# Attention products with values: one matmul over all query tiles for a head's first two key tiles, with three raw weight buffers for four

## The chip, the cores and the metric

The kernel runs on one core of one Trainium2 chip. The metric is device time in microseconds (us) of that core. TensorE (PE, with its weight loads PEld), VectorE (DVE), ScalarE (ACT) and GpSimd (POOL) each take their instructions in a fixed order; SyncE (SP) issues most of the transfers.

## The reference, cut to what matters

Two residual layers over 512 tokens of width 1024, all in float32. The change lies in layer 0, whose mixer has two halves that read one normalised input: gated linear attention (GLA, 4 heads) and block-sparse softmax attention (MoBA, 8 heads of width 64).

```python
def mix_even(h, w_in, w_gate2, b_gate, gla_norm, q_norm, k_norm, w_o):
    proj = h @ w_in
    qa, ka, va, ra, glr, qb, kb, vb = _split(proj, EVEN_SPLITS)
    ...
    oa = rmsnorm(gla_chunked(...), gla_norm).reshape(B, S, GLA_V) * jax.nn.silu(ra)
    ob = moba_attention(rmsnorm(qb, q_norm), rmsnorm(kb, k_norm), vb)
    return jnp.concatenate([oa, ob], axis=-1) @ w_o
```

With 512 tokens and blocks of 256, a MoBA head is softmax over the causal keys of a 512 by 512 score matrix (with a penalty on one block), times the values.

## The kernel before, in words

Activations lie transposed: 128 channels on the partitions, 512 tokens along a row. To keep float32 accuracy every large product is made of three matmuls (`mm3`, L130 to L132), on a high and a low part of each operand. Weights arrive as blocks of 128 x 1024; each lands in a `raw` buffer, ACT casts it into `whi` (L114), and DVE takes the rest into `wlo` (L115).

A MoBA head h has, for its two query halves g = 0 and 1 (two query tiles of 128 each):
- S(h, g) (`s_step`): the scores, and the softmax on DVE, ACT and POOL, which leaves probabilities `p`.
- T(h, g, jj) (`t_step`): PE transposes of the blocks of `p` for the key tiles 2jj and 2jj+1 into the one PSUM bank `ptp`; ACT casts them to the high part of `th`, DVE subtracts for the low part (L711, L712).
- A(h, g, jj) (`a_step`): the products of values and `th` into the one bank `av` (L726). After the last one ACT copies half of `av` to `lo` (L732) and DVE adds into `of` (L733); every second head casts `of` into the operand A (L735, L736).

The three T and the three A of a head are (0,0), (1,0) and (1,1). Between these steps PE does "fills", pieces of six 512-wide matmuls of other projections (`fill`): in order qa, ka, va, the gate's halves ra0 and ra1, and the output projection wob. The class `Plan` decides the order when the program is built: each step has a cost, dependencies with assumed latencies (`LAT`) and PSUM banks; it takes the first step that is due by its own clock, and a fill where none is. PE's order on the chip is this order; it waits where a step comes too early.

When ra0 or ra1 is done, a chain makes its gate `sl` for two 512-wide halves, one after the other through one buffer `ra` (xin[:, 7]): DVE multiplies (L627), ACT does Exp, Ln, Exp (L628 to L630), POOL multiplies (L631); the second half's DVE step waits for the first half's POOL step.

After the MoBA heads comes the GLA stage, planned likewise, for n = 0 to 7: `att` (L799 to L801) makes scores in two `s` banks, which DVE copies under a mask into `atts` (L802); `kt` transposes keys, which ACT copies to `kst` (L810); `ds` (L819) needs `kst`; `o` needs the copied `atts`; ACT normalises its result `ob` (L840 to L850); `otp` (L860) transposes it, and DVE multiplies it by `sl` (L862). The buffers `atts` and `sts` are cleared on POOL (L783, L786), whose order puts these clears behind both multiplies of ra0's gate:

```python
pool.tensor_mul(s1, s1, ra)                 # L631, in ra_g(0), then ra_g(1)
a = gl.tile([P, 2, 2, P], F32, name=f"att{p}")
pool.memset(a, 0.0)                         # L783
```

Of the kernel before, what the change touches and what calls it, by code (L numbers as in the profile page):

```python
# [7 lines left out]
F32 = mybir.dt.float32  # L8
F32R = mybir.dt.float32r
U32 = mybir.dt.uint32  # L10
AF = mybir.ActivationFunctionType
ALU = mybir.AluOpType
AX = mybir.AxisListType

P = 128
S = 512
# [28 lines left out]
def kernel(  # L45
# [13 lines left out]
    act, dve, pool, pe = nc.scalar, nc.vector, nc.gpsimd, nc.tensor  # L59

    cp = ctx.enter_context(tc.tile_pool(name="cp", bufs=1))
    wp = ctx.enter_context(tc.tile_pool(name="wp", bufs=4))
# [21 lines left out]
    A = cp.tile([P, 32, S], F32R, name="A")  # L84
    ident = cn[:, C_ID : C_ID + P]
# [11 lines left out]
    def m_tile(name, tag="tp"):  # L97
        return ps.tile([P, S], F32, tag=tag, name=name, bufs=2 if tag == "s" else 1)
# [5 lines left out]
    def block_parts(n):  # L104
        i = wcount[0]
        wcount[0] += 1
        raw = wp.tile([P, 1024], F32, tag="raw", name=f"raw{i}", bufs=4)
        hi = wp.tile([P, 1024], F32R, tag="whi", name=f"whi{i}")
        lo = wp.tile([P, 1024], F32R, tag="wlo", name=f"wlo{i}")
        ready.append((hi, lo))  # L110
        for q in range(n):
            c = slice(q * 1024 // n, (q + 1) * 1024 // n)
            nc.sync.dma_start(raw[:, c], w[i, :, c])
            act.copy(hi[:, c], raw[:, c])  # L114
            dve.tensor_sub(lo[:, c], raw[:, c], hi[:, c].bitcast(F32))  # L115
            yield

    def emit_block():
        for _ in block_parts(1):
            pass  # L120
# [127 lines left out]
    def gain_rsqrt(out_, vp, n, y0, t):  # L248
        act.activation(y0, vp, AF.Ln, scale=1.0 / n, bias=eps_c)
        act.activation(y0, y0, AF.Exp, scale=-0.5)  # L250
        dve.scalar_tensor_tensor(t, y0, -0.5 / n, y0, op0=ALU.mult, op1=ALU.mult)
        dve.scalar_tensor_tensor(t, vp, n * EPS, t, op0=ALU.add, op1=ALU.mult)
        dve.scalar_tensor_tensor(out_, t, 1.5, y0, op0=ALU.add, op1=ALU.mult)
# [129 lines left out]
    def even_mixer(nrm, nxt):  # L383
# [5 lines left out]
        mp = ms.enter_context(tc.tile_pool(name="mb", bufs=2, reuse_waits="tile"))  # L389
# [7 lines left out]
        for k in range(KT):  # L397
            if k % 2 == 0:
                parts = block_parts(2)
# [39 lines left out]
        vb = [A[:, i : i + 2, :].rearrange("p a (h d) -> p (a h) d", d=P) for i in (16, 18, 24, 26)]  # L439
# [19 lines left out]
        def qk_norm(which, half):  # L459
            o = held[which, half]  # L460
            nm = f"{which}{half}"
            sm = kp.tile([P, 4, 16], F32, tag="sm", name=f"sm_{nm}", bufs=2)
            v, y0, tt, f = (sm[:, i, :].rearrange("p (t h) -> p t h", t=2) for i in range(4))
            sq = mp.tile([P, 2, S], F32, tag="th", name=f"sq_{nm}", bufs=3)
            for j in range(2):
                act.activation(sq[:, j, :], o[j], AF.Square)
                dve.tensor_reduce(v[:, j, :], sq[:, j, :].rearrange("p (h d) -> p h d", d=64), axis=AX.X, op=ALU.add)
            hh = slice(2 * half, 2 * half + 2)
            dve.tensor_mul(v, v, rs2_t[:, hh, None].to_broadcast([P, 2, 8]))
            gain_rsqrt(f, v, 64.0, y0, tt)  # L470
            dve.tensor_mul(f, f, rs_t[:, hh, None].to_broadcast([P, 2, 8]))
            kns = []
            for j in range(2):
                kn = o[j] if which == "k" else mp.tile([P, S], F32, tag="pt", name=f"kn_{nm}{j}", bufs=6)
                dve.tensor_mul(
                    kn.rearrange("p (h d) -> p h d", d=64),
                    o[j].rearrange("p (h d) -> p h d", d=64),
                    f[:, j, :, None].to_broadcast([P, 8, 64]),
                )
                kns.append(kn)  # L480
            held[which, half] = kns
# [33 lines left out]
        for k, half in [(k, h) for k in range(6) for h in range(2)] + [(6, 0), (7, 0), (6, 1), (7, 1)]:  # L515
# [7 lines left out]
            c = slice((k % 2) * S, (k % 2 + 1) * S)  # L523
# [13 lines left out]
        dve.tensor_mul(rs2_t, rs_t, rs_t)  # L537
        rs = nrm.rs()
        qk_norm("k", 0)
        qk_norm("k", 1)  # L540
        o = m_tile("glr", "av")
        for k in range(KT):
            j = k % 3
# [8 lines left out]
        qk_turn("k", (0, 1))  # L552
        pj(1)
        qk_norm("q", 0)
        pj(1)
        qk_turn("k", (2, 3))
# [31 lines left out]
        for h in range(2):  # L588
            a, b = halves[h], halves[1 - h]
# [7 lines left out]
        for p in range(4):  # L597
            pj(1)
            for t in range(2):
                for h in range(2):  # L600
                    c = t * 16 + 4 * p + 2 * h
                    pe.matmul(gps[:, c : c + 2], qS[p][h][:, (2 + t) * P : (3 + t) * P], km[:, 2 * p + h, :], start=True,
                              stop=True)
# [55 lines left out]
        hs = {}  # L659

        def s_step(h, g):
# [9 lines left out]
            for i in (2 * g, 2 * g + 1):  # L671
# [23 lines left out]
                dve.tensor_scalar(pt[:, :n], pt[:, :n], ac[:, 3:4], None, op0=ALU.mult)  # L695
                hs[h, i] = pt

        def t_step(h, g, jj):
            tp = m_tile(f"ptp_{h}_{g}{jj}")
            w_ = 512 if jj < g else 384  # L700
            c = 0
            spans = []
            for j in (2 * jj, 2 * jj + 1):
                c0 = c
                for i in (2 * g, 2 * g + 1):
                    if i >= j:
                        pe.transpose(tp[:, c : c + P], hs[h, i][:, j * P : (j + 1) * P], ident)  # L707
                        c += P
                spans.append((j, c0, c))
            th = mp.tile([P, 2, S], F32R, tag="th", name=f"th_{h}_{g}{jj}", bufs=3)  # L710
            act.copy(th[:, 0, :w_], tp[:, :w_])  # L711
            dve.tensor_sub(th[:, 1, :w_], tp[:, :w_], th[:, 0, :w_].bitcast(F32))  # L712
            hs[h, g, jj] = th, spans

        def a_step(h, g, jj):
            p, hh = divmod(h, 2)
            if g == 0:
                hs["av"] = m_tile(f"av{h}", "av")
                if hh == 0:
                    hs["of"] = mp.tile([P, S], F32, tag="of", name=f"of{p}")  # L720
            av = hs["av"]
            th, spans = hs[h, g, jj]
            for j, c0, c1 in spans:
                q0 = (2 * g + 2) * P - (c1 - c0)
                for u in range(2):
                    pe.matmul(av[:, q0 : (2 * g + 2) * P], vb[j][:, h, :], th[:, u, c0:c1], start=j == 0 and u == 0,  # L726
                              stop=j == 2 * g + 1 and u == 1)
            if g == 1 and jj == 1:
                r = slice(64 * hh, 64 * hh + 64)
                of = hs["of"]  # L730
                lo_ = mp.tile([64, S], F32, tag="lo", name=f"lo{h}", bufs=1)
                act.copy(lo_, av[64:128, :])  # L732
                dve.tensor_add(of[r, :], av[0:64, :], lo_)  # L733
                if hh == 1:
                    act.copy(A[:, 16 + 4 + p, :], of)  # L735
                    dve.tensor_sub(A[:, 24 + 4 + p, :], of, A[:, 16 + 4 + p, :].bitcast(F32))  # L736
# [4 lines left out]
        at = []  # L741

        def add_s(h, g):
            k = 2 * h + g - 3
            deps = [(("T", k // 2, k % 2, k % 2), 0.0)] if k >= 0 else []
            at.append((("S", h, g), 0.45 if g == 0 else 0.75, deps, ("s", 2, LB), lambda: s_step(h, g)))

        def add_t(h, g, jj):
            at.append((("T", h, g, jj), 0.4, [(("S", h, g), LS)], ("tp", 1, LT), lambda: t_step(h, g, jj)))

        def add_a(h, g, jj):
            deps = [(("T", h, g, jj), LA)]
            if g == 0 and h > 0:
                deps.append((("A", h - 1, 1, 1), LV))
            if g == 1:
                deps.append((("A", h, 0, 0) if jj == 0 else ("A", h, 1, 0), 0.0))
            at.append((("A", h, g, jj), 0.45 if g == 0 else 0.75, deps, None, lambda: a_step(h, g, jj)))

        add_s(0, 0)
        add_s(0, 1)  # L760
        for h in range(8):
            add_t(h, 0, 0)
            if h < 7:
                add_s(h + 1, 0)
            add_a(h, 0, 0)
            add_t(h, 1, 0)
            if h < 7:
                add_s(h + 1, 1)
            add_a(h, 1, 0)
            add_t(h, 1, 1)  # L770
            add_a(h, 1, 1)
# [9 lines left out]
        for p in range(2):  # L781
            a = gl.tile([P, 2, 2, P], F32, name=f"att{p}")
# [190 lines left out]
    n0 = Norm("n0", V_MIX)  # L973
    n1 = Norm("n1", V_MLP)
    even_mixer(n0, n1)
    n2 = Norm("n2", V_MIX + 8)
    mlp(0, n1, n2)
# [126 lines left out]
```

## Time and profile before

| | |
|---|---|
| median of 3 runs | 1079.29 us (1079.22 to 1080.67) |
| the profiled execution | 1080.98 us, of which the span from first to last instruction is 1079.2 us |
| PE busy | 1072.1 us, 99% of the span, 4970 matmuls |
| DVE, ACT, POOL busy | 546.0, 411.7, 102.4 us |
| MoBA heads | about 88 to 180 us of the span |
| GLA stage | about 180 to 222 us of the span |

Busy shares are averages over the whole span. The two MLPs and the odd layer, behind 230 us, are long runs of equal matmuls; the stage of the change is dense in short steps on four engines. A PE matmul's printed duration overlaps its successor's: what a matmul takes from the stream is the distance between two starts.

### The profile page before, as it was taken

The page shows a single profiled execution, that of the slowest core. Times are in us where ns is not written, and L with a number is a line of the kernel's source. Part 1 is how long each engine was busy: PE and PEld are TensorE (multiplying, and loading weights), DVE is VectorE, ACT ScalarE, POOL GpSimd, SP SyncE. Part 2 cuts the span into 40 slices and gives each one's busy share as a digit, 9 for nine tenths or more (in the row PEclk, how much of TensorE's full clock was granted, in tenths as well). Part 3 has the DMA queues.
Part 4 walks back from the last instruction along what each step waited for, and adds up shares of the span by engine and source line. Part 5 has one row for each costly group of instructions (what it writes and reads, how often), then busy time and mean ns, then how long its engine had stood idle before and what let it go on. Part 6 is the DMA issues. An engine that isn't in the chain of part 4 may idle for free.

```text
span 1079.2 us, 12499 instructions
## 1 busy us (share of the span) xinstructions
PE 1072.1 (99%) x4970; PEld 885.7 (82%) x4970; DVE 546.0 (51%) x767; ACT 411.7 (38%) x597; POOL 102.4 (9%) x113
## 2 busy tenths in 40 slices
PE   9999999999999999999999999999999999999998
PEld 7778888788888888888888888888888888888887
DVE  7788885676444344334334864555443344344331
ACT  6565575755342133124123333334342133133110
POOL 0244432012000000000002100121000000000000
PEclk9999999999999999999999999999999999999999
DMA  8123123123322323333233232332333322322221
GB/s 305 43 78 103 54 90 126 60 78 98 98 98 98 98 98 98 97 98 98 98 98 98 89 97 98 98 98 98 98 98 98 97 98 97 96 96 94 94 72 59
DMA packets 31179, 104.77 MB, mean 97 GB/s; under 512 B 3633, under 2 KB 4498, under 8 KB 31122
## 3 DMA queue, kind: packets, MB, share of 16 engines
q1 hardware_dynamic: 30050, 101.46, 28.8%
q0 software_dynamic: 640, 2.10, 0.6%
q8 instruction: 39, 0.64, 0.3%
q10 hardware_dynamic: 432, 0.42, 0.1%
q14 instruction: 18, 0.15, 0.0%
HBM read 101.87 MB, written 2.10 MB: 96 GB/s over the span
## 4 chain that ended last, share of the span: by engine, by line
PE 95%; DVE 2%; ACT 1%; DMA 0%; issue 0%; DVEq 0%; ACTq 0%
PE m L130 22%; PE m L132 22%; PE m L131 21%; PE wo L130 1%; PE wo L132 1%; PE wo L131 1%; PE av L726 1%; PE ptp L707 1%; PE kb L130 1%; PE kb L132 1%; PE kb L131 1%; PE va L130 1%; PE va L132 1%; PE xc L130 1%; PE va L131 1%; PE xc L132 1%
## 5 line engine op out<-in xcount | busy, mean ns | idle before, releaser
L114 ACT CAST whi<-raw 128x1024 fp32r<-128x1024 f32 (+1 forms) x188 | 194.1, 1034 | 528.0 <-PE m L131 432.0
L115 DVE TENSOR_TENSOR wlo<-raw,whi 128x1024 fp32r<-128x1024 f32 (+1 forms) x188 | 227.2, 1209 | 191.6 <-ACT whi L114 191.5
L132 PE MATMUL m<-A,wlo 128*128 128x512 f32 x768 | 298.8, 389 | 0.0
L131 PE MATMUL m<-A,whi 128*128 128x512 f32 x768 | 298.8, 389 | 0.0
L130 PE MATMUL m<-A,whi 128*128 128x512 f32 x768 | 298.8, 389 | 0.0
L132 PEld LDWEIGHTS m<-A,wlo 128*128 128x128 f32 x768 | 144.2, 188 | 30.1
L130 PEld LDWEIGHTS m<-A,whi 128*128 128x128 f32 x768 | 144.2, 188 | 29.8
L131 PEld LDWEIGHTS m<-A,whi 128*128 128x128 f32 x768 | 144.2, 188 | 29.7
L131 PE MATMUL m<-E,whi 128*128 128x512 f32 (+1 forms) x264 | 101.0, 383 | 0.0
L132 PE MATMUL m<-E,wlo 128*128 128x512 f32 (+1 forms) x264 | 101.0, 383 | 0.0
L130 PE MATMUL m<-E,whi 128*128 128x512 f32 (+1 forms) x264 | 101.0, 383 | 0.0
L292 DVE TENSOR_TENSOR x<-x,m 128x1024 f32<-128x1024 f32 x31 | 37.8, 1221 | 109.1 <-PE m L132 109.1
L331 DVE SCALAR_TENSOR_TENSOR r<-m,rs_n 128x1024 f32<-128x1024 f32 x32 | 39.2, 1224 | 96.8 <-PE m L132 96.8
L273 POOL TENSOR_TENSOR ss_n<-ss_n,sq_n 128x512 f32<-128x512 f32 x21 | 32.8, 1561 | 418.5 <-ACT sq_n L271 417.8
L131 PEld LDWEIGHTS m<-E,whi 128*128 128x128 f32 x264 | 49.6, 188 | 9.8
L132 PEld LDWEIGHTS m<-E,wlo 128*128 128x128 f32 x264 | 49.6, 188 | 9.7
L130 PEld LDWEIGHTS m<-E,whi 128*128 128x128 f32 x264 | 49.6, 188 | 9.5
L332 ACT ACTIVATE r<-r 128x1024 f32<-128x1024 f32 x32 | 34.0, 1062 | 19.9 <-DVE r L331 19.9
L335 DVE TENSOR_TENSOR E<-r,E 128x1024 fp32r<-128x1024 f32 x16 | 19.6, 1226 | 17.2 <-ACT E L334 17.2
L260 DVE SCALAR_TENSOR_TENSOR A<-x,vc,A 128x512 fp32r<-128x512 f32 x24 | 27.3, 1140 | 1.3
L335 DVE TENSOR_TENSOR A<-r,A 128x1024 fp32r<-128x1024 f32 x16 | 19.6, 1225 | 15.1 <-ACT A L334 15.1
L131 PE MATMUL wo<-A,whi 128*128 128x512 f32 x64 | 24.9, 389 | 0.0
(303 smaller groups left out, 1401.7 us busy)
## 6 DMA issues: line engine op xcount, KB each, us to landing
raw<-in_w_dram SPq DMA_DIRECT2D x180, 512.0 KB, 3.3
raw<-in_w_dram SPq DMA_DIRECT2D x8, 256.0 KB, 5.3
x<-in_xT_dram POOLq DMA_DIRECT2D x8, 256.0 KB, 5.8
xin<-in_xT_dram SPq DMA_DIRECT2D x7, 256.0 KB, 5.5
out_dram<-x SPq DMA_DIRECT2D x7, 256.0 KB, 2.1
cd<-in_cond_dram SPq DMA_DIRECT2D x1, 608.0 KB, 6.3
pw<-in_poolw_dram ACTq DMA_DIRECT2D x1, 256.0 KB, 2.5
out_dram<-x SPq DMA_DIRECT2D x2, 128.0 KB, 1.7
```

What stands on the lines that cost most here:

```text
L114: act.copy(hi[:, c], raw[:, c])
L115: dve.tensor_sub(lo[:, c], raw[:, c], hi[:, c].bitcast(F32))
L130: pe.matmul(o, w_hi, a_hi, start=start, stop=False)
L131: pe.matmul(o, w_hi, a_lo, start=False, stop=False)
L132: pe.matmul(o, w_lo, a_hi, start=False, stop=stop)
L260: dve.scalar_tensor_tensor(A[:, 8 + k, c], src[:, k, c], col(gcol + k), A[:, k, c].bitcast(F32), op0=ALU.mult, op1=ALU.subtract)
L273: (pool if buf is None else dve).tensor_add(ss, ss, sq)
L292: dve.tensor_add(x[:, 2 * n : 2 * n + 2, :], x[:, 2 * n : 2 * n + 2, :], o)
L331: dve.scalar_tensor_tensor(r, o, 0.0, bc2(st["rs"]), op0=ALU.max, op1=ALU.mult)
L332: act.activation(r, r, AF.Square)
L335: dve.tensor_sub(lo, r, hi.bitcast(F32))
L707: pe.transpose(tp[:, c : c + P], hs[h, i][:, j * P : (j + 1) * P], ident)
```

## The change

For each head the products with the first two key tiles are no longer made once for each query half. One tile `th` per head (a single buffer) collects the transposed blocks of key tiles 0 and 1 for all four query tiles, over T(h,0,0) and T(h,1,0); the step A(h,1,0) then does key tile 0 over 512 columns (two pieces of 256 in `th`, addressed as one operand) and key tile 1 over 384. A(h,0,0) is gone. T(h,1,1) and A(h,1,1) stay, in a tile of their own with two buffers. The plan's costs and dependencies follow. In memory, `raw` has three buffers for four, and the squares in `qk_norm` move from the `th` buffers to the two `of` buffers.

```diff
-        raw = wp.tile([P, 1024], F32, tag="raw", name=f"raw{i}", bufs=4)
+        raw = wp.tile([P, 1024], F32, tag="raw", name=f"raw{i}", bufs=3)
...
-            sq = mp.tile([P, 2, S], F32, tag="th", name=f"sq_{nm}", bufs=3)
             for j in range(2):
+                sq = mp.tile([P, S], F32, tag="of", name=f"sq_{nm}{j}")
...
+            if (g, jj) == (0, 0):
+                hs["th"] = mp.tile([P, 2, 10 * P], F32R, tag="th", name=f"th_{h}", bufs=1)
+            if jj == 0:
+                th = hs["th"][:, :, 3 * P * g : 3 * P * g + w_]
+            else:
+                th = mp.tile([P, 2, 3 * P], F32R, tag="th1", name=f"th1_{h}", bufs=2)
...
-            if g == 0:
+            if jj == 0:
                 hs["av"] = m_tile(f"av{h}", "av")
...
+                th = hs["th"]
+                parts = [
+                    (0, lambda u: th[:, u, :].rearrange("p (a b) -> p a b", a=2)[:, :, 0 : 2 * P], 0),
+                    (1, lambda u: th[:, u, 2 * P : 5 * P], P),
+                ]
...
-                    pe.matmul(av[:, q0 : (2 * g + 2) * P], vb[j][:, h, :], th[:, u, c0:c1], start=j == 0 and u == 0,
-                              stop=j == 2 * g + 1 and u == 1)
+                    pe.matmul(av[:, q0:S], vb[j][:, h, :], view(u), start=j == 0 and u == 0, stop=j == 3 and u == 1)
...
-            at.append((("A", h, g, jj), 0.45 if g == 0 else 0.75, deps, None, lambda: a_step(h, g, jj)))
+            at.append((("A", h, g, jj), 0.85 if jj == 0 else 0.46, deps, None, lambda: a_step(h, g, jj)))
...
-            add_a(h, 0, 0)
```

The plan's order changes with it. On PE, at the passage from the last MoBA head to the GLA stage, the program of before has these rows (`ra_1610` is ra0, `ra_1793` is ra1, `av_1721` and `av_1820` belong to heads 6 and 7; "..." leaves out rows of the same fill, of a transposing step or of the same `att`):

```order
L132 MATMUL ra_1610<-A,wlo_1372 128x512
L726 MATMUL av_1721<-th_11_1747,A 128x256 x2
L726 MATMUL av_1721<-th_11_1747,A 128x128 x2
L130 MATMUL ra_1793<-A,whi_1612 128x512
...
L726 MATMUL av_1820<-th_00_1766,A 128x256 x2
...
L726 MATMUL av_1820<-th_10_1811,A 128x256 x4
...
L726 MATMUL av_1820<-th_11_1839,A 128x128 x2
L799 MATMUL att_1897<-xin,G 64x64
```

and the changed program these (`ra_1663` is ra0, `ra_1781` is ra1, `av_1776` head 7):

```order
L132 MATMUL ra_1663<-A,wlo_1428 128x512
L737 MATMUL av_1776<-th_1712,A 128x512 x2
L737 MATMUL av_1776<-th_1712,A 128x384 x2
L130 MATMUL ra_1781<-A,whi_1665 128x512
...
L737 MATMUL av_1776<-th_7_1756,A 128x256 x2
L737 MATMUL av_1776<-th_7_1756,A 128x128 x2
L808 MATMUL att_1825<-xin,G 64x64
...
L828 MATMUL ds_1847<-xin,kst 64x128 x2
L808 MATMUL att_1852<-xin,G 64x64
```

The plan takes five fills fewer among the heads. Before, ra0's last matmul stands ahead of head 6's last product, and six fills, two T and head 7's three A lie between it and the first `att`; now only head 7's two products and one fill of six matmuls lie between.

On ACT, the rows of before from the second half of ra0's gate (`sl_1775`) on:

```order
L628 ACTIVATE sl_1775<-xin 128x512
L629 ACTIVATE sl_1775<-sl_1775,one_c 128x512
L630 ACTIVATE sl_1775<-sl_1775 128x512
L711 CAST th_11_1839<-ptp_11_1835 128x384
L114 CAST whi_1972<-raw_1971 128x1024
L732 COPY lo_1870<-av_1820 64x512
L735 CAST A<-of_1722 128x512
L810 COPY kst<-kt_1907 128x512
```

and of the changed program (`sl_1765`):

```order
L742 COPY lo_1798<-av_1776 64x512
L628 ACTIVATE sl_1765<-xin 128x512
L629 ACTIVATE sl_1765<-sl_1765,one_c 128x512
L745 CAST A<-of_1690 128x512
L630 ACTIVATE sl_1765<-sl_1765 128x512
L819 COPY kst<-kt_1835 128x512
```

The last transposed block of head 7 is now cast ahead of the gate, and the copy to `kst` that `ds` needs stands directly behind the gate's last Exp. POOL's order is the same row for row: ra0's two multiplies, then the clears of `atts` and `sts`.

On DVE, where the first product with ra1's gate stands, before (`xin<-ra_1793` is the second half of that gate, `sl_1944` the gate):

```order
L627 TENSOR_TENSOR xin<-ra_1793,rs_n_345 128x512
L251 SCALAR_TENSOR_TENSOR osm_1988<-osm_1988 128x2
...
L862 SCALAR_TENSOR_TENSOR ob_0_2045<-otp_2042,vc,sl_1775 128x256
...
L251 SCALAR_TENSOR_TENSOR osm_2061<-osm_2061 128x2
...
L862 SCALAR_TENSOR_TENSOR ob_1_2121<-otp_2118,vc,sl_1944 128x256
L865 TENSOR_TENSOR A<-ob_1_2121,A 128x2x128
```

and now (`ra_1781`, `sl_2004`; `osm_2050` belongs to the norm of `ob` 2):

```order
L627 TENSOR_TENSOR xin<-ra_1781,rs_n_345 128x512
L811 COPY_PREDICATED att_1816<-cd,att_2062 128x128
L811 COPY_PREDICATED att_1816<-cd,att_2067 128x128
L251 SCALAR_TENSOR_TENSOR osm_2050<-osm_2050 128x2
L871 SCALAR_TENSOR_TENSOR ob_1_2081<-otp_2078,vc,sl_2004 128x256
L252 SCALAR_TENSOR_TENSOR osm_2050<-osm_2050 128x2
L811 COPY_PREDICATED att_1820<-cd,att_2103 128x128
L253 SCALAR_TENSOR_TENSOR osm_2050<-osm_2050 128x2
```

Before, 22 DVE instructions stood between ra1's second half and the first product with its gate; now three do, and that product stands in the middle of the norm of `ob` 2, which `otp` 2 needs.

## Rows read from the trace of the kernel before

**Rows 1.** The page: busy times; the chain that ended last, by engine

```profile
PE 1072.1 (99%) x4970; PEld 885.7 (82%) x4970; DVE 546.0 (51%) x767; ACT 411.7 (38%) x597; POOL 102.4 (9%) x113
...
PE 95%; DVE 2%; ACT 1%; DMA 0%; issue 0%; DVEq 0%; ACTq 0%
```

**Rows 2.** Timeline of PE (start us, us, instruction): scores and products with values, MoBA heads

```profile
98.01 0.34 PE L677 MATMUL s<-kk,A 128*128 128x384 f32 x1
...
98.84 0.39 PE L130 MATMUL qa<-A,whi 128*128 128x512 f32 x1
...
100.23 0.64 PE L726 MATMUL av<-th,A 128*128 128x256 f32 x4
100.70 0.49 PE L707 MATMUL ptp<-cn,p 128*128 128x128 f32 x3
...
169.54 0.56 PE L726 MATMUL av<-th,A 128*128 128x256 f32 x4
169.94 0.45 PE L130 MATMUL ra<-A,whi 128*128 128x512 f32 x1
170.22 0.39 PE L131 MATMUL ra<-A,whi 128*128 128x512 f32 x1
```

**Rows 3.** Timeline of DVE: ra0's gate, the first masked copies

```profile
169.74 0.69 DVE L627 TENSOR_TENSOR xin<-ra,rs_n 128x512 f32<-128x512 f32 x1 [0.27 <-PE ra L132]
...
175.01 0.69 DVE L627 TENSOR_TENSOR xin<-ra,rs_n 128x512 f32<-128x512 f32 x1 [1.22 <-POOL sl L631]
...
183.19 0.49 DVE L802 COPY_PREDICATED att<-cd,att 128x128 f32<-128x128 uint32 x2
```

**Rows 4.** Timeline of POOL: second multiply of ra0's gate, first clear

```profile
177.87 1.30 POOL L631 TENSOR_TENSOR sl<-sl,xin 128x512 f32<-128x512 f32 x1 [2.89 <-ACT sl L630]
179.10 0.52 POOL L783 MEMSET att<- 128x512 f32 x1
```

**Rows 5.** Timeline of PE: first att, first ds, second att

```profile
180.49 0.27 PE L799 MATMUL att<-xin,G 64*64 64x64 f32 x1
...
183.22 0.44 PE L819 MATMUL ds<-xin,kst 128*64 128x128 f32 x4 [0.30 <-ACT kst L810]
...
183.58 0.27 PE L799 MATMUL att<-xin,G 64*64 64x64 f32 x1
```

**Rows 6.** Timeline of ACT: last Exp of ra0's gate, copy to kst

```profile
177.16 0.64 ACT L630 ACTIVATE sl<-sl 128x512 f32<-128x512 f32 x1
...
182.57 0.59 ACT L810 COPY kst<-kt 128x512 f32<-128x512 f32 x1
```

**Rows 7.** Timelines of DVE and POOL: ra1's gate, first and last step

```profile
185.98 0.69 DVE L627 TENSOR_TENSOR xin<-ra,rs_n 128x512 f32<-128x512 f32 x1 [1.33 <-PE ra L132]
...
193.73 1.30 POOL L631 TENSOR_TENSOR sl<-sl,xin 128x512 f32<-128x512 f32 x1 [3.19 <-ACT sl L630]
```

**Rows 8.** Timelines of PE, DVE and ACT: otp 1 to the next fill; product with sl; scaling of ob

```profile
201.37 0.38 PE L860 MATMUL otp<-cn,ob 128*128 128x128 f32 x2
...
202.95 0.50 PE L130 MATMUL wob<-A,whi 128*128 128x512 f32 x1
...
201.86 0.48 DVE L862 SCALAR_TENSOR_TENSOR ob<-otp,vc,sl 128x256 f32<-128x256 f32 x1 [1.16 <-PE otp L860]
...
205.37 0.69 ACT L850 ACTIVATE ob<-ob,osm 128x128 f32<-128x128 f32 x2
```

**Rows 9.** Busy time by window: length, PE, PEld, DVE, ACT, POOL; the GLA stage

```profile
180.40:222.00 41.60, 41.05 (x294) 31.62 (x294) 26.46 (x74) 30.08 (x98) 3.65 (x4) 1.00 0.20 64
```

**Rows 10.** Timelines of PE and DVE: T(1,0,0), the late subtraction behind it

```profile
104.63 0.52 PE L707 MATMUL ptp<-cn,p 128*128 128x128 f32 x3
...
107.37 0.54 DVE L712 TENSOR_TENSOR th<-ptp,th 128x384 fp32r<-128x384 f32 x1
```

**Rows 11.** Waits of the SP queue: transfers of raw blocks

```profile
SPq L113 <- DVE wlo L115: 895.8, 169, 19.4
```

**Rows 12.** Timeline of PE: a 512-wide matmul near the start

```profile
9.12 0.63 PE L132 MATMUL kb<-whi,A 128*128 128x512 f32 x1
```

More of the change, by code (lines that the diff above doesn't have):

```diff
@@ L463, in qk_norm @@
             v, y0, tt, f = (sm[:, i, :].rearrange("p (t h) -> p t h", t=2) for i in range(4))
-            sq = mp.tile([P, 2, S], F32, tag="th", name=f"sq_{nm}", bufs=3)
             for j in range(2):
-                act.activation(sq[:, j, :], o[j], AF.Square)
-                dve.tensor_reduce(v[:, j, :], sq[:, j, :].rearrange("p (h d) -> p h d", d=64), axis=AX.X, op=ALU.add)
+                sq = mp.tile([P, S], F32, tag="of", name=f"sq_{nm}{j}")
+                act.activation(sq, o[j], AF.Square)
+                dve.tensor_reduce(v[:, j, :], sq.rearrange("p (h d) -> p h d", d=64), axis=AX.X, op=ALU.add)
             hh = slice(2 * half, 2 * half + 2)
@@ L696, in s_step @@
                 hs[h, i] = pt
+        blocks_of = {
[3 rows of a table added]
+        }
         def t_step(h, g, jj):
             tp = m_tile(f"ptp_{h}_{g}{jj}")
[L700 to L713, printed above, removed]
+            bl = blocks_of[g, jj]
+            for c, (j, i) in enumerate(bl):
+                pe.transpose(tp[:, c * P : (c + 1) * P], hs[h, i][:, j * P : (j + 1) * P], ident)
+            w_ = len(bl) * P
+            if (g, jj) == (0, 0):
[4 more added lines that the diff above has]
+                th = mp.tile([P, 2, 3 * P], F32R, tag="th1", name=f"th1_{h}", bufs=2)
+                hs["th1"] = th
+            act.copy(th[:, 0, :], tp[:, :w_])
+            dve.tensor_sub(th[:, 1, :], tp[:, :w_], th[:, 0, :].bitcast(F32))
         def a_step(h, g, jj):
             p, hh = divmod(h, 2)
-            if g == 0:
+            if jj == 0:
                 hs["av"] = m_tile(f"av{h}", "av")
@@ L720, in a_step @@
                     hs["of"] = mp.tile([P, S], F32, tag="of", name=f"of{p}")
+                th = hs["th"]
[3 more added lines that the diff above has]
+                ]
+            else:
+                th1 = hs["th1"]
+                parts = [(2, lambda u: th1[:, u, 0 : 2 * P], 2 * P), (3, lambda u: th1[:, u, 2 * P : 3 * P], 3 * P)]
             av = hs["av"]
-            th, spans = hs[h, g, jj]
-            for j, c0, c1 in spans:
-                q0 = (2 * g + 2) * P - (c1 - c0)
+            for j, view, q0 in parts:
                 for u in range(2):
-                    pe.matmul(av[:, q0 : (2 * g + 2) * P], vb[j][:, h, :], th[:, u, c0:c1], start=j == 0 and u == 0,
-                              stop=j == 2 * g + 1 and u == 1)
+                    pe.matmul(av[:, q0:S], vb[j][:, h, :], view(u), start=j == 0 and u == 0, stop=j == 3 and u == 1)
             if g == 1 and jj == 1:
@@ L752, in add_a @@
             deps = [(("T", h, g, jj), LA)]
-            if g == 0 and h > 0:
+            if jj == 0 and h > 0:
                 deps.append((("A", h - 1, 1, 1), LV))
-            if g == 1:
-                deps.append((("A", h, 0, 0) if jj == 0 else ("A", h, 1, 0), 0.0))
-            at.append((("A", h, g, jj), 0.45 if g == 0 else 0.75, deps, None, lambda: a_step(h, g, jj)))
+            if jj == 1:
+                deps.append((("A", h, 1, 0), 0.0))
+            at.append((("A", h, g, jj), 0.85 if jj == 0 else 0.46, deps, None, lambda: a_step(h, g, jj)))
         add_s(0, 0)
```

3 rows, old and new, of the table blocks_of are left out of this document.

## The prediction

> **What bounds the kernel now.** I read the page first. PE is busy for 99% of the span and holds 95% of the chain that ended last [rows 1]: the time is the sum of PE's stream, and a wait of PE adds to it in full. So two questions decide: what the new products take from the stream, and whether PE, in its new order, meets a result that isn't ready. I then read the timelines of PE, DVE, POOL and ACT from 88 to 222 us, the stage whose order changes; there PE hardly waits, and the one wait that matters below is 0.30 us of `ds` for `kst`.
>
> **The products.** What counts is start to start. A(0,0) and A(1,1), two of 256 and two of 128 columns, take 0.40 (169.54 to 169.94), A(1,0), four of 256, takes 0.47 [rows 2]. The new A(1,0) is two of 512 and two of 384; the scores hold exactly these four, 98.01 to 98.84, 0.83 [rows 2]. So a head goes from 0.40 + 0.47 to 0.83 (the A(1,1) is kept): 0.04 saved, for the number of columns stays and only short matmuls go. The 128-wide end of a step also costs what follows: after A the first fill matmul took 0.28 to the next start (169.94 to 170.22) where 0.23 is usual (0.83 holds two of these) [rows 2]; that is 0.05 where a fill followed A(0,0). So 0.04 to 0.12 a head, 0.3 to 1.0 for eight. **I take -0.7.** The operand in two pieces of 256 shows in no row; four of 256 at 0.47 against 0.46 for two of 512 bounds it at 0.01 each, nothing here.
>
> **The passage to GLA.** This is the large term. The order rows show that ra0 now ends just ahead of head 7's products. Let r be the start of the DVE step that opens ra0's gate, 169.74 before [rows 3]; PE's next matmul behind ra0 starts at 169.54, r - 0.20 [rows 2]. The gate's chain ran from there to the end of POOL's second multiply, 177.87 + 1.30 = 179.17, 9.43 us; the clear of the first `atts` followed at once, 179.10 + 0.52 = 179.62, r + 9.9 [rows 4]. Before, PE came to the first `att` at 180.49, r + 10.75 [rows 5]: the chain was done, and cost nothing. What hid it was 10.95 us of PE work: head 6's last product, 36 fill matmuls, two T and head 7's three A.
> Now PE has, from r - 0.20: A(1,0) 0.83, six fill matmuls at 0.23 = 1.38, A(1,1) and the step into `att` 0.50. So it comes to the first `att` at r + 2.5. The second `att` starts 3.09 behind the first, 0.30 of it that wait [rows 5], so at r + 5.3 if nothing holds it. But it writes the two `s` banks that the first `att` filled; they come free by DVE's masked copies into `atts`, and these need POOL's clear, which POOL makes behind both multiplies. Clear at r + 9.9, a copy of about a quarter us (two take 0.49 [rows 3]) and a tenth to start PE: r + 10.2. PE loses 4.9, of which 0.3 was lost before: **+4.6**.
> The same wait is met a little earlier in another form: `ds`, at r + 4.9, needs `kst`, whose copy on ACT (0.59) now stands behind the gate's last Exp, which ended at 177.16 + 0.64, r + 8.1 [rows 6]. So `ds` goes at about r + 8.7, and the second `att` then waits for the rest. The two overlap; only the later one counts.
> Bounds: the second half of the chain ran with little between its steps, 175.01 to 179.17, 4.16 [rows 3, 4]; twice that is 8.32, 1.1 less than measured, and the net loss falls to 3.5. The cast of `of` now stands between the Ln and the last Exp; at 0.6 (`kst`'s copy of the same width, 0.59 [rows 6]) it raises it to 5.2.
>
> **The second gate.** ra1 now ends late in the GLA stage. Its chain ran from 185.98 to 193.73 + 1.30 = 195.03, 9.05 us [rows 7]; the first product with it came at 201.86 [rows 8], so nobody waited. Call its start r1. PE's new path from r1 - 0.20 to `otp` 2 is `ds` 0.36 (183.22 to 183.58 [rows 5]) and a fill, twice: 2 x (0.36 + 1.45); `o` and `att` 1.36 and a fill 1.45; `otp`, `o`, `att` 1.58 (201.37 to 202.95 [rows 8], some 0.2 of it `otp`) and a fill 1.45 (1.38 and the slower first): r1 + 9.3. But DVE's product with the gate, 0.48, can't start before r1 + 9.05; behind it on DVE stands the norm of `ob` 2, then its scaling on ACT, 0.69 [rows 8]. With a cast and the small steps between, `ob` 2 is there at about r1 + 10.6, and `otp` 2 waits 1.3. ACT does not win this back soon: it was already busy for 30.08 of the stage's 41.60 us [rows 9], and from r1 on it has the six steps of ra1's gate on top of seven norms, whose copies, squares and scalings are now late together; `otp` 3 needs the next of them. Bounds: 0.9 (ACT catches up at once) to 4. I take the middle, **+2.5**.
>
> **The heads.** Five fills fewer stand among them, so DVE and ACT have less time for the same softmax. T holds the one `ptp` bank until DVE's subtraction: the latest in the heads ended 107.37 + 0.54 - 104.63 = 3.28 behind T's start [rows 10]. In the new order the closest T follow one another after twelve fill matmuls (2.8 plus T's own 0.3) or after scores, products and six fills, again about 3.1. Most subtractions are sooner by a us or more, so a few waits of 0.1 to 0.3: bounds 0 to 1.5, **I take +0.2**. The single `th` is no wait on PE: head h+1's first cast into it comes a fill behind A(1,0) of head h.
>
> **What is hidden.** A raw transfer waited for DVE's `wlo` in 169 cases [rows 11]: it leaves as soon as a buffer frees. With three buffers it leaves one block later, and a block is 24 matmuls of 0.23, 5.5 us, of the roughly 16 that it is early; nothing, unless transfers took ten us longer. The squares in two `of` buffers are each reduced before the next but one is made: nothing.
>
> **The sum.** -0.7 + 4.6 + 2.5 + 0.2 = +6.6 on the profiled execution's 1080.98, 1087.6. That run is 1.7 above the median of 1079.29; on the median it gives 1085.9. As the second gate is the softest term and the before's own small waits late in GLA may go in it, I take **1085.3**.
>
> **A rule on the clock.** A 512-wide matmul printed 0.63 at 9.12 us, near the start [rows 12], and 0.39 at 98.84 [rows 2]: the first is the lower level (1.2 GHz), the second 2.4. No row shows PE standing still behind the start for the 3.8 us that `ds` would wait, so none says whether the clock stays. The Trainium skill, "TensorE: Matmul & The Clock Gate", section on HAM oscillation, holds that a PE left idle is throttled to half its clock and has to warm up again. By the rows alone the sum is +6.6; by that rule it would be some 2 to 4 more.
>
> **Rivals.**
> 1. *The clock falls in the wait.* For it: a low level at the start [rows 12]. Against: `ds` splits the standstill. If it stays low for 4 to 9 us (at the start it was low still at 9.12), about 10 to 20 fill matmuls lose 0.2 each: 2 to 4, so 1087 to 1089.5.
> 2. *The gate is not what holds `att`*, the other side: if the first masked copy found its clear done by r + 4.9, PE would not stop, and the savings alone remained: 1078.6, with the second gate at its lower bound 1079.5, no change. Against: even the close-packed chain takes 8.32 and the clear follows it.
> 3. *Only the first passage costs.* ACT and DVE have caught up by `otp` 3: +0.9 for the second gate, 1084.3, or with the close-packed chain 1082.9.
> 4. *DVE becomes the bound in the heads*: T waits at most heads, its upper bound of 1.5 and more: 1087.
>
> **How the numbers follow.** Both passages cost, as summed: 0.50. Rival 3: 0.23. Rival 4: 0.07. Rival 1: 0.10. Rival 2: 0.07. Savings larger than any row allows: 0.03. The range from 1081.5 to 1088.5 holds the first three and half of rival 1; it spans the bounds of the passage (3.5 to 5.2) and of the second gate (0.9 to 4). A measurement can tell 0.2%, 2.2 us, from no change. Slower 0.87; the same 0.09 (rival 2, and a small passage); faster 0.04.
>
> **What would show it.** Right: a wait of PE of 3 to 4 us at the first `ds`, named for the copy to `kst`, another of about 1 at the second `att` for the masked copy, POOL's clears behind the second multiply, some us of waits at `otp` 2 and 3 for `ob`. The A steps of a head at 1.23 for 1.27. Wrong: PE without a wait behind head 7, or T waiting in most heads.

## The result, and the profile after

The changed kernel takes 1090.32 us (median of 4, 1088.58 to 1091.71) where before takes 1079.26; over all runs the ratio is 1.0096 (1.0084 to 1.0108), slower by 0.96%. The profiled execution took 1091.71 us, its span 1089.9, 10.7 more than the span of before.

One thing is needed to read the times: executions of one kernel fall into two groups some 1.8 us apart, by how long the stretch from the first `kb` to the first `rs_tp` takes at the start (some 24 or 22.2 us in the traces), with before at 1079.2 and some 1081.0 and the changed kernel at 1088.58 and 1090.2 or more. Like for like, in the lower group, the loss is 9.4 us. Spans of two traces are compared stage by stage below.

The waits of PE in the changed kernel, in order of size (waited for, us in total, times, longest):

```profile
PE ds L828 <- ACT kst L819: 3.2, 1, 3.2
PE otp L869 <- ACT ob L859: 3.1, 3, 1.4
...
PE att L808 <- DVE att L811: 1.1, 1, 1.1
...
PE ptp L708 <- DVE th L718: 0.4, 1, 0.4
```

Before had 0.3 of the first of these [rows 5], 0.2 of the second and nothing of the rest. The timeline of PE from head 7's first product to the first `o`:

```profile
171.38 0.97 PE L737 MATMUL av<-th,A 128*128 128x512 f32 x4
172.19 0.39 PE L130 MATMUL ra<-A,whi 128*128 128x512 f32 x1
...
173.56 0.57 PE L737 MATMUL av<-th,A 128*128 128x256 f32 x4
174.06 0.27 PE L808 MATMUL att<-xin,G 64*64 64x64 f32 x1
...
179.63 0.44 PE L828 MATMUL ds<-xin,kst 128*64 128x128 f32 x4 [3.15 <-ACT kst L819]
181.16 0.36 PE L808 MATMUL att<-xin,G 64*64 64x64 f32 x1 [1.09 <-DVE att L811]
...
182.32 0.77 PE L130 MATMUL ra<-A,whi 128*128 128x512 f32 x1
182.90 0.63 PE L131 MATMUL ra<-A,whi 128*128 128x512 f32 x1
...
187.74 0.40 PE L130 MATMUL ra<-A,whi 128*128 128x512 f32 x1
...
188.44 0.61 PE L847 MATMUL o<-xin,att 128*128 128x128 f32 x4
```

Head 7's new product takes 0.81 to the next start, where the scores' four of the same widths take 0.83 [rows 2], so its operand in two pieces costs nothing. The two bracketed starts are the waits the prediction named. Behind them a fill matmul prints 0.63 for 0.39 until 187.7: this is the lower clock. By window (length, then PE, PEld, DVE, ACT, POOL busy; PEclk is the column behind POOL):

```profile
172.00:180.00 8.00, 4.85 (x39) 3.70 (x37) 3.57 (x5) 5.91 (x10) 2.24 (x2) 1.00 0.21 68
180.00:184.00 4.00, 2.91 (x20) 2.42 (x19) 1.00 (x4) 0.90 (x3) 2.59 (x5) 0.59 0.00 0
184.00:188.00 4.00, 4.00 (x24) 2.51 (x24) 0.50 (x2) 0.52 (x2) 0.00 (x0) 0.56 0.00 0
188.00:200.00 12.00, 12.00 (x95) 8.54 (x93) 7.45 (x23) 7.53 (x23) 0.00 (x0) 1.00 0.13 46
...
180.70:187.60 6.90, 6.44 (x39) 4.62 (x40) 1.50 (x6) 1.42 (x5) 1.89 (x4) 0.51 0.00 0
```

The last line is the whole of the low stretch.

What PE waited for stands in the timelines of DVE, ACT and POOL; DVE's step at 171.58 opens ra0's gate:

```profile
171.58 0.69 DVE L627 TENSOR_TENSOR xin<-ra,rs_n 128x512 f32<-128x512 f32 x1 [0.32 <-PE ra L132]
...
178.35 0.62 ACT L630 ACTIVATE sl<-sl 128x512 f32<-128x512 f32 x1
179.00 0.59 ACT L819 COPY kst<-kt 128x512 f32<-128x512 f32 x1
...
179.05 1.26 POOL L631 TENSOR_TENSOR sl<-sl,xin 128x512 f32<-128x512 f32 x1 [3.26 <-ACT sl L630]
180.25 0.52 POOL L792 MEMSET att<- 128x512 f32 x1
...
180.81 0.50 DVE L811 COPY_PREDICATED att<-cd,att 128x128 f32<-128x128 uint32 x2 [1.65 <-POOL att L792]
```

With r = 171.58, `kst` was copied at r + 7.4 to 8.0, the clear ended at r + 9.2, the second `att` started at r + 9.6.

The second gate, in the timelines of POOL, DVE and PE: the last multiply of ra1's gate, the product that needs it, and the three waits of `otp`:

```profile
205.84 1.28 POOL L631 TENSOR_TENSOR sl<-sl,xin 128x512 f32<-128x512 f32 x1 [3.19 <-ACT sl L630]
...
207.15 0.48 DVE L871 SCALAR_TENSOR_TENSOR ob<-otp,vc,sl 128x256 f32<-128x256 f32 x1
...
208.46 0.62 PE L869 MATMUL otp<-cn,ob 128*128 128x128 f32 x2 [0.69 <-ACT ob L859]
...
212.31 0.62 PE L869 MATMUL otp<-cn,ob 128*128 128x128 f32 x2 [0.97 <-ACT ob L859]
...
224.57 0.62 PE L869 MATMUL otp<-cn,ob 128*128 128x128 f32 x2 [1.41 <-ACT ob L859]
```

Before, the product came 6.8 us after the multiply had ended [rows 7, 8]; now it goes as the multiply ends (205.84 + 1.28 = 207.12). The three waits are those of `otp` 2, 3 and 7.

In the heads one T waits visibly, T(3,1,1) on PE, for DVE's late subtraction of T(3,1,0) (two rows of PE, one of DVE):

```profile
126.98 0.60 PE L708 MATMUL ptp<-cn,p 128*128 128x128 f32 x4
...
130.76 0.55 PE L708 MATMUL ptp<-cn,p 128*128 128x128 f32 x3 [0.45 <-DVE th L718]
...
130.02 0.68 DVE L718 TENSOR_TENSOR th<-ptp,th 128x512 fp32r<-128x512 f32 x1
```

Summed over all heads from start to start in the two traces, the steps that begin with a product took 10.42 us before and 9.84 now: 0.58 saved. The 21 steps from a fill to a T took 6.04, 0.288 each; before, 12 of them took 0.244 each: 21 x 0.044 = 0.9 lost.

Where the 10.7 went, from PE's starts in the two traces (the changed kernel takes 30 fill matmuls, five fills, fewer before the first `att` and 30 more behind; a fill matmul is 0.228):

| stretch | before | after | net |
|---|---|---|---|
| to the first score | 86.72 | 86.95 | +0.2 |
| first score to first `att` (30 fewer, 6.83) | 93.77 | 87.11 | +0.2 |
| first `att` to second `att` | 3.09 | 7.10 | +4.0 |
| second `att` to first `o` | 4.54 | 7.28 | +2.7 |
| first `o` to first `woa` (30 more) | 34.35 | 44.77 | +3.6 |

The first row's 0.2 is no more than executions differ by: the traces of runs 8 to 10 below, the same program up to there, have 86.61 to 87.06.

### The profile page after: what moved, and what is told of

It is laid out like the page before. It is cut to its first block, busy times and chain, and to the rows that moved or that the text cites. A ratio compares the mean times of both kernels' runs of the same rounds, so it can differ in the third digit from the quotient of the medians.

```text
span 1089.9 us, 12422 instructions
## 1 busy us (share of the span) xinstructions
PE 1075.2 (99%) x4938; PEld 885.0 (81%) x4938; DVE 547.0 (50%) x767; ACT 412.5 (38%) x597; POOL 102.1 (9%) x113
## 4 chain that ended last, share of the span: by engine, by line
PE 92%; DVE 4%; ACT 2%; issue 1%; POOL 1%; DMA 0%; ACTq 0%
PE m L130 21%; PE m L132 21%; PE m L131 21%; PE wo L132 1%; PE wo L130 1%; PE wo L131 1%; PE kb L130 1%; PE kb L132 1%; PE kb L131 1%; PE ra L130 1%; PE xc L130 1%; PE xc L132 1%; PE bg L132 1%; PE bg L130 1%; PE cg L130 1%; PE u L130 1%
```

## The experiments

Theory after the traces: five fills that stood between ra0's gate and GLA now stand at its end; so the passage waits (4.0), the standstill takes the clock (2.7 in the trace), ra1's gate comes late (3.6), and the new products themselves are worth -0.6 with some 0.9 of T waits against it. Rivals: the third raw buffer, the products, or a late ACT and DVE cause the loss. Where weights are wanted in another order, the blocks are read in that order (the table `FILL`, not shown). Each group of runs had its own runs of before.

**1. The third raw buffer alone** (kernel before).

```diff
-        raw = wp.tile([P, 1024], F32, tag="raw", name=f"raw{i}", bufs=4)
+        raw = wp.tile([P, 1024], F32, tag="raw", name=f"raw{i}", bufs=3)
```

> The kernel before with three raw buffers for four, nothing else changed. By the account of the traces the third buffer costs nothing behind the start; at the start the first scores came 0.23 us later in the changed kernel, which may be its doing. Expected: 0 to +0.3 us against before, no new wait of PE behind the start. Rival (the buffer is part of the 10.7 us): +1 or more, with PE waiting for whi or wlo.

Measured: 1079.28, ratio 0.9994 (0.9985 to 1.0003), no new wait. The buffer costs nothing here, nor in run 8, which has it together with the moved squares.

**2. The old products, ra0 four fills later** (kernel before).

```diff
-        def ra_g(r2):
-            o = yield from t_unit_g(f"ra{r2}", H)
+        def ra_g(r2, g=None):
+            o = yield from g or t_unit_g(f"ra{r2}", H)
...
-            yield from ra_g(0)
-            yield from ra_g(1)
+            r1 = t_unit_g("ra1", H)
+            for _ in range(4):
+                yield next(r1)
+            yield from ra_g(0)
+            yield from ra_g(1, r1)
```

> The kernel before with its old products and its old number of fills; only four of ra1's fills are made ahead of ra0, so that ra0 ends four fills later, two fills ahead of the first att. If the loss comes from the place of ra0's end and not from the new products, PE now comes to the first att some 3.2 us behind the start of ra0's gate, not 10.75, and the passage costs about 3.3 us of waits at ds and the second att; if the standstill also lowers the clock, another 2 to 3, in all +5 to +6. Without the clock +3.3. Rival (the new products themselves cost): 0 to +0.3.

Measured: 1086.02, ratio 1.0050 (1.0037 to 1.0064); 1084.15 in the lower group, +4.9. Its waits of PE:

```profile
PE ds L823 <- ACT kst L814: 2.6, 1, 2.6
...
PE att L803 <- DVE att L806: 1.1, 1, 1.1
```

Up to the first `att` it runs as before (180.57 against 180.49); from there to the first `o` it takes 12.63 for 7.63, +5.0: 3.4 of new waits and 1.6 behind them, where PEclk is 0.69 (186 to 190) and 0.88 (190 to 194). The old products lose in the same place; the cause is where ra0 ends.

**3. ra0 ahead of va** (changed kernel).

```diff
+            yield from ra_g(0)
             yield from tok_g("va", va_evac)
             held["proj"] = True
-            yield from ra_g(0)
             yield from ra_g(1)
```

> The changed kernel with the fills in the order qa, ka, ra0, va, ra1, so that ra0's gate is done long before the passage; all products and the number of fills among the heads stay. Expected by the account (passage 4.0, low clock behind it 2.7, second gate 3.6): the passage and the clock go, the second gate stays: about -6.7 against the changed kernel, 1083.6, PEclk 1.00 from 180 to 190 us. If the slow clock had another cause than the wait: -4. If the second gate's loss is itself a late effect of the passage: -10.

Measured: 1084.42, ratio 1.0046 (1.0033 to 1.0059). PEclk is 1.00 from 172 to 190 us, and the waits are:

```profile
PE otp L870 <- ACT ob L860: 3.0, 3, 1.4
PE ptp L709 <- DVE th L719: 1.8, 2, 1.3
...
PE ds L829 <- ACT kst L820: 0.6, 1, 0.6
```

From span to span it gains 5.5, not 6.7 (4.2 in the lower group): passage and clock are gone, and 0.9 is given back at T, where ra0's gate now falls among the softmaxes. The second gate stands alone and has the same three waits of 0.70, 0.96 and 1.39.

**4. Zeros in the wait** (changed kernel; the matmuls add zero; `held["unit"]` is the open PSUM tile of ra1).

```diff
+        held["unit"] = o
...
+            if n == 0:
+                for _ in range(7):
+                    pe.matmul(held["unit"][:, 0, 0:256], warm[:, 0:P], warm, start=False, stop=False)
             dp_ = m_tile(f"ds_{n}", "av")
```

> The changed kernel with seven matmuls of zeros (128x256 in float32, about 0.43 us each at 2.4 GHz, 3.0 in all) put ahead of the first ds, adding zero to ra1's sum: PE works where it stood still for 3.15 us. Nothing becomes ready sooner. If the standstill lowers the clock, the clock stays at 1.00 from 180 to 188 us and the kernel gains about 2.7 against the changed kernel, though PE does more work. If the clock falls for another reason, or the second att's wait of 1.1 does it: 0, or a little slower.

Measured: 1087.13, 1.0071 (1.0058 to 1.0084) of before; 1087.0 in the lower group, 1.6 less than the changed kernel's 1088.58; trace against trace 2.7. The same windows as above:

```profile
172.00:180.00 8.00, 7.84 (x52) 6.25 (x50) 3.46 (x5) 5.81 (x10) 2.34 (x2) 1.00 0.20 68
180.00:184.00 4.00, 2.94 (x36) 2.17 (x36) 1.00 (x4) 0.97 (x4) 2.49 (x5) 1.00 0.00 0
184.00:188.00 4.00, 4.00 (x40) 3.09 (x31) 1.82 (x4) 2.73 (x9) 0.00 (x0) 1.00 0.00 0
```

Nothing was ready sooner (`ds` 179.53 for 179.63, and `att` still waits 1.1), yet the kernel is faster: the standstill took the clock, and its 1.1 us at `att` alone did not.

**5. Both gates ahead of va** (changed kernel).

```diff
+            yield from ra_g(0)
+            yield from ra_g(1)
             yield from tok_g("va", va_evac)
             held["proj"] = True
-            yield from ra_g(0)
-            yield from ra_g(1)
```

> The changed kernel with the fills in the order qa, ka, ra0, ra1, va: both gates are begun and ended among the heads, and nothing of either stands at the passage. By the account (passage 4.0, clock 1.4 to 2.7, second gate 3.6 gone; products -0.6, T waits +1.0 left) the time is that of before within 0.5 us: -0.6 to +0.8, so 1079 to 1080 where before is 1079.3, and no wait of otp for ob over 0.3. If the second gate's loss is that GLA has too few fills and not the gate: +3.6 stays, and about 1083.

Measured: 1086.63, ratio 1.0064 (1.0052 to 1.0077). The expectation failed. The waits:

```profile
PE otp L870 <- ACT ob L860: 3.9, 1, 3.9
PE ptp L709 <- DVE th L719: 2.7, 3, 1.3
```

va's last seven fills and one of wob are forced ahead of the first `att`, so that GLA runs out of them: its last `otp` waits 3.94 with nothing left to do, and the clock falls there (PEclk 0.65 from 228 to 232 us). And both gates delay T in the heads. It says nothing on the second gate's loss; it says that fills are what GLA lives on.

**6. ra1's gate without the sigmoid** (changed kernel).

```diff
+                if r2 == 1:
+                    dve.tensor_mul(s1, o[:, j, :], rs)
+                    continue
                 dve.tensor_mul(ra, o[:, j, :], rs)
```

> The changed kernel; of ra1's gate the sigmoid is left out (no Exp, Ln, Exp on ACT, no product on POOL: DVE writes ra1 times rs straight into sl), so the output is another one. PE's order stays. If ra1's chain (three passes on ACT, 512 wide, twice) holds ob 2 and its successors back, the waits of otp go and with them 3.6: about -3.6 against the changed kernel. If only the place of the product with the gate in DVE's order matters, or ACT is late without it: -1 or less. The passage stays as it is, 4.0 and the slow clock.

Measured: 1088.10, 1.0070 (1.0058 to 1.0083) of before. The first `o` to the first `woa` takes 42.76 for 44.77: 2.0 of the 3.6 is the chain, and `otp` 2 and 3 no longer wait; `otp` 7 still does, 1.30. From the first `att` to the first `o` it takes 13.06 with the same waits as the changed kernel's 14.38. The lower clock cost 1.4 here and 2.7 there, for the low stretch is shorter:

```profile
180.90:184.40 3.50, 3.31 (x19) 2.79 (x20) 0.83 (x4) 0.89 (x3) 1.62 (x3) 0.51 0.00 0
```

**7. The clears on DVE** (changed kernel).

```diff
-            pool.memset(a, 0.0)
+            dve.memset(a, 0.0)
```

> The changed kernel with the two clears of atts on DVE instead of POOL, so that they no longer wait for ra0's second multiply. The prediction says that ds's wait for kst and the second att's wait overlap and only the later counts: then ds still waits 3.1 and the second att nearly not, -0.9 to -1.1 against the changed kernel. If the clock falls only because of the second standstill, another -1.4 to -2.7. If the second att waits for the same time on something else: 0.

Measured: 1087.93, 1.0074 (1.0060 to 1.0088) of before; 0.7 less than the changed kernel in the lower group. `ds` still waits 3.2 and the second `att` 0.4, for 1.1. So the clear behind the gate held the second `att`, and what its wait added behind `ds`'s is what went; that `ds`'s wait would be no gain by itself was not run. The clock falls all the same (0.85 from 176 to 180, 0.72 to 184): `ds`'s wait with a short one behind it was enough.

**8. The five fills put back ahead of GLA** (changed kernel).

```diff
-            add("ATT", 0.6, [(("O", n - 4), 0.0)] if n > 3 else [], ("s", 2, GA), g_att)
+            add("ATT", 0.6, [(("O", n - 4), 0.0)] if n > 3 else [("ra0", 8.5)], ("s", 2, GA), g_att)
...
-                add_n("KT", 4 * n, 0.11 * min(4, 6 - 4 * n), [], ("tp", 1, GK), g_kt)
+                add_n("KT", 4 * n, 0.11 * min(4, 6 - 4 * n), [("ra0", 8.5)], ("tp", 1, GK), g_kt)
```

> The changed kernel, in whose plan the first att and kt now wait for ra0 with 8.5 us: five of the fills that the changed kernel leaves to the end of GLA stand ahead of the first att, and the order of GLA is that of before, row for row. If the loss is the place of the fills (passage 4.0, the clock behind it 1.4 to 2.7, second gate 3.6), it goes whole: what stays is -0.6 for the products, +1.0 for T and up to 0.2 at the start, so +0.2 to +0.6 against before, no wait over 0.4 behind 160 us, clock 1.00. If the new products slow GLA in another way: +2 or more. In the run without ra1's sigmoid 1.6 of the second gate's 3.6 stayed; if that part has a cause of its own, +1.6 stays here.

Measured: 1080.69, ratio 1.0000 (0.9991 to 1.0009); lower group 1079.0 to 1079.2. All of the loss is gone, `otp` 7's part too, which so had no cause of its own. The passage is even shorter than before's, 7.14 from the first `att` to the first `o` for 7.63: 0.3 of it is `ds`'s old wait. Waits behind 86 us:

```profile
PE ptp L708 <- DVE th L718: 0.4, 1, 0.4
...
PE otp L869 <- ACT ob L859: 0.3, 1, 0.3
```

**9. Three of the five** (changed kernel; 6.0 for 8.5 in both lines).

> The same with 6.0 us: three fills ahead of the first att, two are left for the end. ds comes 9.0 us behind the start of ra0's gate (kst was there at 8.0), the second att at 9.4 (its banks came free at 9.6). Expected +0.2 to +0.6 against before as with five fills, and 0 to 0.2 more for the second att; if three don't cover, a wait of ds or att of 0.5 or more and a lower clock.

Measured: 1082.95, ratio 1.0020 (1.0011 to 1.0029). The passage is covered (`att` waits 0.2, PEclk 1.00), but the expectation left out GLA: `otp` waits for `ob` 1.2 in two places, and the kernel loses 2. With two fills fewer ahead of GLA, ra1 ends later in it: its gate opens 10.4 us behind the first `att`, where run 8 has 5.0.

**10. Three fills, and one ahead of each of two T** (changed kernel; as 9, and the plan holds `ptp` for 2.9 us, not `LT`, behind the steps in `TW`, so that a fill goes ahead of the next T).

```diff
+TW = ((3, 1, 0), (6, 1, 0))
...
-            at.append((("T", h, g, jj), 0.4, [(("S", h, g), LS)], ("tp", 1, LT), lambda: t_step(h, g, jj)))
+            at.append((("T", h, g, jj), 0.4, [(("S", h, g), LS)], ("tp", 1, 2.9 if (h, g, jj) in TW else LT), lambda: t_step(h, g, jj)))
```

> The same with 6.0 us, and one fill more ahead of the two T that waited longest (T(3,1,1) some 0.57, T(6,1,1) some 0.26). If the T waits are what keeps the new products from a gain, they fall from 1.0 to about 0.3, and the kernel is 0.3 to 0.6 faster than before: -0.4 or so; a difference this small may not be told from none. If DVE is simply late in the heads, the waits move to the next T: +0.2 to +0.6 as without.

Measured: 1086.19, ratio 1.0041 (1.0027 to 1.0054), slower where a gain was expected. T's waits are gone, but the plan counts its 6.0 us from ra0, which now ends earlier, and puts no fill between head 7's last product and the first `att`. `kst`'s copy then comes only at r + 12.1, behind head 7's cast of `of` on ACT and not behind the gate, whose last Exp ended at r + 8.3 (r = 169.49 here; the waits of PE, then two rows of ACT):

```profile
PE otp L870 <- ACT ob L860: 3.3, 3, 1.5
...
PE ds L829 <- ACT kst L820: 1.1, 1, 1.1
...
180.96 0.62 ACT L746 CAST A<-of 128x512 fp32r<-128x512 f32 x1 [1.53 <-DVE of L744]
181.60 0.59 ACT L820 COPY kst<-kt 128x512 f32<-128x512 f32 x1
```

The waits behind the heads cost more than those in them did, and the clock falls again (PEclk 0.68 from 196 to 200, behind 1.45 and 0.58 at `otp` 0).

**11. 46 fills ahead of GLA, one of them at T(3,1,1)** (changed kernel; 9.8 for 8.5, `TW = ((3, 1, 0),)`).

> The changed kernel with 46 fills ahead of the first att, as many as before, divided otherwise than in the run with 8.5: one goes ahead of T(3,1,1), the plan then puts two more at later T by itself, and two stand ahead of the first att. GLA's order is that of before. If the T waits (1.0 in the heads) are what eats the products' 0.6, most of them go and nothing is lost later: 0.4 to 0.9 less than with 8.5 alone, so -0.3 to -0.8 against before. If DVE or ACT is late in the heads anyway, the waits move: +0.0 to +0.2.

Measured: 1080.27, ratio 0.9996 (0.9987 to 1.0005); lower group 1078.75, 0.5 under before's 1079.25. Over all runs this is not told from no change.

**12. The same with T(6,1,1)** (9.8, `TW` as in 10).

> The same with a fill ahead of T(6,1,1) too, 46 fills in all, one ahead of the first att. In the run with 6.0 us and both T all T waits were gone (fill to T took 0.245 on the mean, 0.244 before), but two fills too few stood ahead of GLA and the waits there came back. Expected with 46: -0.6 to -0.9 against before, no wait at ds over 0.5. If ds waits for kst because only one fill stands behind head 7: +1 to +3.

Measured: 1078.18 against 1079.31, ratio 0.9988 (0.9979 to 0.9997): 0.12% or 1.1 us faster than before, and the only kernel here whose interval lies below 1. Its lower group ends at 1078.36, under before's lowest of 1079.16; its upper one ends at 1080.08, under before's 1080.73. The largest waits of PE; neither `ds`, `att` nor `ptp` is among them:

```profile
PE warmup L395 <- DVE warm L79: 1.2, 1, 1.2
PE tp_k L488 <- DVE kl L498: 1.0, 1, 1.0
PE kb L131 <- ACT A L260: 0.6, 1, 0.6
PE tp_q L488 <- DVE kn_q L476: 0.3, 1, 0.3
PE otp L870 <- ACT ob L860: 0.2, 1, 0.2
```

A fill now takes 0.245 to a T, as before, and PEclk is 1.00 from 176 to 190 us. Some 0.65 of the gain is the products' (9.77 for 10.42, start to start), some 0.5 the shorter passage of run 8; the kernel before was not run with a plan that counts from the gate, so how much of the 0.5 it could have alone is open.

## Why the prediction was wrong

It had the sign, the places and the mechanism of both waits; 1085.3 was 5.0 too low, and 1090.3 lies above its range, as the lowest run does by 0.1. Some 1.7 of the 5.0 is the groups: the forecast was set on before's lower one, and three of the four runs fell in the upper. Like for like 3.3 are missing. Its steps:

- **The clock, left out of the sum with "`ds` splits the standstill" (rival 1, chance 0.10):** this is the step that failed. PE stood for 3.15 us and, one `ds` of 0.44 later, for 1.09, and the granted clock went to 0.51, the lower of its two levels, from 180.7 to 187.6 us: `ds` between the waits did not keep it up. Run 4 shows that the standstill did it. It cost 2.7 us in the profiled execution and 1.4 to 1.6 where other runs show it (runs 2, 4, 6); rival 1 had 2 to 4. By the Trainium skill, "TensorE: Matmul & The Clock Gate", section on HAM oscillation, an idle PE is throttled to half its clock. The traces agree for these two waits, with the 0.51; behind the single wait of 1.41 at `otp` 7 the clock stayed at 1.00 (222 to 232 us).
- **The second gate, +2.5:** +3.6, behind the clock the term furthest off. The mechanism was right for 2.0 of it (run 6): the product with the gate went at r1 + 9.0, `otp` 2 waited 0.69 for the 1.3 foretold, `otp` 3 another 0.97. A third wait of 1.4 at `otp` 7 was not foreseen; it comes with the place of the fills (run 8 has none).
- **The heads, +0.2:** some +0.9. T waited at intervals of two fills behind late subtractions; the bound of 1.5 held, the value was too small.
- **The passage, +4.6:** +4.0. Right, with both waits where they were foretold: `ds` 3.15 at r + 8.05 (foretold r + 8.7), `att` at r + 9.6 (r + 10.2). The gate's chain took 8.7 us for the 9.4 carried over from before. That only the later wait counts is borne out by run 7 for the second one.
- **The products, -0.7:** -0.6. Right; runs 11 and 12 turn them into a gain.
- **What is hidden, nothing:** right (runs 1 and 8).
- **The sum:** the trace's +6.6, 1085.9 on before's median, was then cut to 1085.3 because before's own small waits might go in it; they did not. With its terms as measured it is -0.6 + 0.9 + 4.0 + 2.7 + 3.6 + 0.2 (the start), 10.8 for 10.7; with the clock at 1.4 it is 9.5 for the 9.4 of the lower group. Rival 3's second figure, 1082.9, is 1083.2 by the prediction's own terms.

Rivals 2 and 3 were wrong: the gate held `ds` and `att`, and ACT had not caught up by `otp` 3. Rival 4 was not it, though T's waits are real. Over the span the granted clock is 0.996 in the profiled execution and 0.998 in the changed kernel's three others, as in the traces of runs 2, 6 and 7 with their shorter low stretch; that the 2.7 was 1.4 there is inferred from this and the times. Even the fall itself varies: of run 10's five executions, one has 1.000 and 1082.94 us, the others 0.998 and 1084.35 or more. Why the clock stays low for longer, or does not fall, in one execution of a program and not in the next stays open.

## What to carry to other kernels

Where a planner sets the order, a saving that makes one stage need less filler moves that filler elsewhere: count the filler between a long chain's start and its first user, before and after, and where a wait appears there, look for a lower granted clock behind it and price that too. The new products were good all along; they paid once the plan knew the latency of ra0's gate and the fills stood where they covered a wait. A plan must name every dependency that isn't short: this one had none from the gate to the first `att`.

## What the runs showed that was not expected

Matmuls of zeros in a wait made the kernel faster by 1.6 us (run 4); run 4's own expectation had this, the prediction had not. Work between two waits did not keep the clock: it fell behind waits of 3.15 and 0.38 us (run 7), of 2.6 and 1.1 (run 2), and of 1.45 and 0.58 (run 10, in four of five executions), with short matmuls between them. Single waits left it at 1.00: 1.1 (run 4), 1.41 (`otp` 7 of the changed kernel), and 0.70 and 0.96 some 4 us apart (run 3). One of 3.94 took it (run 5).
